# Counts, normalising steps and probabilities moved to ScalarE, and select() interleaved two tiles at a time with pair 0

## The chip, the cores and the metric

The kernel runs on one core of a Trainium2 chip. The metric is the device time of one launch in microseconds. A core has five engines that run side by side, each with its own instruction queue, worked off in order: TensorE (PE; its weight loads are PEld), VectorE (DVE), ScalarE (ACT), GpSimd (POOL) and SyncE (SP), which issues the DMAs. An instruction that waits for a semaphore holds everything behind it in its own queue.

## The reference

The program is a decoder trunk of two layers over 1024 positions of 1024 channels, all in float32. In each layer one projection of the normalised, modulated input is split into a convolution branch and an attention branch:

```
p = h @ w_in[l]
u_val, u_gate, g_conv, c_q, c_kv, k_idx, w_idx, g_attn = split(p)
y_conv = conformer_conv(...) * silu(g_conv)     # gate, causal conv of width 31, layer norm, silu, @ w_pw2
y_attn = dsa_attention(...) * silu(g_attn)
x = x + gate * rmsnorm(concat(y_conv, y_attn) @ w_out[l])
```

In the attention, an indexer gives every query t a score for every key s ≤ t. The 256 keys of the highest score are kept (of equal ones those with the lower position), and 8 heads attend to these alone:

```
_, sel = lax.top_k(score, 256)
logits = q . kv[sel] / sqrt(128) + rel_bias[t5_bucket(t - sel)]
o = softmax(logits) @ kv[sel]
```

## The kernel before

**Top 256 by bisection.** The 1024 queries are 8 tiles of 128. The first two have at most 256 keys and keep them all. For the other six, called j = 0 to 5, with 384, 512, 640, 768, 896 and 1024 keys, `topk` finds the 256th highest score of each query bit by bit. The upper half of a score's bits lies as int16 in `pl`. `search` tries a candidate per bit and counts the keys on one side of it: the counts of j = 1, 3, 5 on DVE (L559: 512, 768 and 1024 keys), those of j = 0, 2, 4 on ACT (L554, a Sign whose sum is the count). POOL then takes the step to the next candidate (L549, L562, L564, L566). Search 1 has 15 bits, search 2 has 16. Between them is the mid-search: for each tile, DVE counts the keys above the found upper half (L586) and puts the lower half of those equal to it in `pl` (L588), and the counts are added to the threshold `thr` (L592). L602 on ACT puts the scores back in place.

**Flags.** `select(j)` makes of the found value `tf` the mask of the kept keys, in place of the scores: greater (L608) and equal (L612), a running count of the equal ones (L613), those within the number needed (L614), all on DVE; their sum on POOL (L615) and the final 0 or −BIG on ACT (L616).

**Beside search 2**, PE works through products in an order written by hand: gate projections `g`, the transposes `zt` of the normalised convolution output, the pointwise products `pw`, `v`, and the queries `uq`. The other engines serve it: DVE takes the statistics (L693) and normalises `An` (L720, 32 tiles of 128x128, after a power on POOL, L717, that comes eight times for four tiles each); ACT applies silu to `zt` (L764, `sl`) and to the gates (L742); `sl` is split into a rounded high part `silh` (L767, a cast on DVE) and the rest `sill` (L768, POOL); DVE multiplies the pointwise products by the gate, `yc` (L786). Weights are split into high and low parts by ACT (L132) and by POOL or DVE (L133).

**Attention.** `attention` goes through four pairs of heads. A pair has four blocks c of two query tiles i = 2c, 2c+1: for each head e of the pair, `probs` makes logits (PE `lg`), takes a maximum with bias and mask (DVE L843, L847), the exponential and its sum (ACT L850), the reciprocal (DVE L851), and the multiplication by it (POOL L852). PE transposes the result (L865), ACT and DVE empty PSUM (L870, L872), and PE multiplies with `v` (`av`, L893, its end taken over by DVE in L896). `select(0)` to `select(3)` stand ahead of the attention in program order, `select(4)` and `select(5)` behind blocks c = 0 and c = 1 of pair 0. Tiles i = 0 and 1 need no flags; tile i needs those of j = i − 2.

**What sets the order.** PE's order is written by hand. The queues of the other engines come from a scheduler that builds them ahead of the launch from the program order and its own clock. Within search 2 a small planner, `Pace`, keeps a clock of DVE (`pace[0].free`): each helper operation registers its duration and the earliest place (`pace[0].op(..., us, lag)`, `pace[0].pe(us)` for PE's progress), and each count of L559 asks `pace[0].count` behind which of them it must be issued. So a helper operation that no longer registers moves the counts' places too. The queues are fixed at launch.

## Time and profile before

| | |
|---|---|
| three runs, median (lowest to highest) | 1235.27 us (1234.69 to 1236.12) |
| the profiled execution | 1234.0 us, of which the span of the records is 1232.2 us |
| PE busy in the span | 1173.8 us (95%) |
| DVE, ACT, POOL busy | 897.0, 701.9, 606.5 us |
| search 2 | layer 0: 262 to 353 us; layer 1: 861 to 954 us |
| pair 0, from the first flag to its last `av` | layer 0: 353.4 to 423.4 us; layer 1: 954.6 to 1025.7 us |

The span runs from the first to the last record; 1.8 us of the execution lie around it. An engine counts as busy while one of its instructions runs, also where it is slowed by another engine. Line numbers are those of the kernel before.

### The profile page before, as it was taken

The page shows a single profiled execution, that of the slowest core. Times are in us where ns is not written, and L with a number is a line of the kernel's source. Part 1 is how long each engine was busy: PE and PEld are TensorE (multiplying, and loading weights), DVE is VectorE, ACT ScalarE, POOL GpSimd, SP SyncE. Part 2 cuts the span into 40 slices and gives each one's busy share as a digit, 9 for nine tenths or more (in the row PEclk, how much of TensorE's full clock was granted, in tenths as well). Part 3 has the DMA queues.
Part 4 walks back from the last instruction along what each step waited for, and adds up shares of the span by engine and source line. Part 5 has one row for each costly group of instructions (what it writes and reads, how often), then busy time and mean ns, then how long its engine had stood idle before and what let it go on. Part 6 is the DMA issues. An engine that isn't in the chain of part 4 may idle for free.

```text
span 1232.2 us, 23069 instructions
## 1 busy us (share of the span) xinstructions
PE 1173.8 (95%) x7832; PEld 975.8 (79%) x7832; DVE 897.0 (73%) x2182; ACT 701.9 (57%) x1616; POOL 606.5 (49%) x1218
## 2 busy tenths in 40 slices
PE   6999999999987999999999999999999599999998
PEld 3788888877875777789989888888798377777998
DVE  4657788898798656757686688898888876667214
ACT  4545767766864556643254376785687355566221
POOL 4431136547548548635483211553864665685222
PEclk9999999999998999999999999999999699999999
DMA  9520258852100001148651122894111000021205
GB/s 352 201 85 18 69 195 274 275 171 75 35 27 1 9 10 47 33 127 292 235 196 34 46 52 74 270 289 160 58 30 43 1 10 5 6 77 63 76 18 189
DMA packets 93158, 130.20 MB, mean 106 GB/s; under 512 B 41576, under 2 KB 70768, under 8 KB 93040
## 3 DMA queue, kind: packets, MB, share of 16 engines
q1 hardware_dynamic: 93040, 128.73, 32.5%
q8 instruction: 62, 1.02, 0.3%
q14 instruction: 56, 0.46, 0.1%
HBM read 115.06 MB, written 13.64 MB: 104 GB/s over the span
## 4 chain that ended last, share of the span: by engine, by line
PE 85%; DVE 5%; POOL 5%; issue 2%; ACT 1%; DMA 1%; SPq 0%; DVEq 0%; POOLq 0%; ACTq 0%
PE av L893 7%; PE pt L865 5%; PE ixs L476 5%; PE u L112 5%; PE u L113 5%; PE u L114 5%; PE g L112 5%; PE g L114 4%; PE g L113 4%; PE o L112 4%; PE o L113 4%; PE o L114 4%; PE lg L112 3%; PE cv L674 2%; PE lg L113 2%; PE lg L114 2%
## 5 line engine op out<-in xcount | busy, mean ns | idle before, releaser
L559 DVE TENSOR_SCALAR_CACHE_REDUCE jv<-pl,cand 128x768 int8<-128x768 uint16 (+1 forms) x186 | 187.9, 1010 | 30.8 <-POOL cand L566 20.0
L554 ACT ACTIVATE ja<-pl,cand 128x896 int8<-128x896 uint16 (+1 forms) x186 | 154.1, 829 | 60.6 <-POOL cand L566 45.7
L850 ACT ACTIVATE p<-p,mx 128x128 f32<-128x128 f32 (+7 forms) x128 | 98.7, 771 | 57.1 <-DVE mx L847 49.1
L852 POOL TENSOR_SCALAR p<-p,ri 128x128 f32<-128x128 f32 (+7 forms) x128 | 99.6, 784 | 39.6 <-DVE ri L851 39.2
L133 POOL TENSOR_TENSOR wul<-raw,wuh 128x342 fp32r<-128x342 f32 (+1 forms) x48 | 46.9, 1000 | 129.3 <-ACT wuh L132 123.3
L112 PE MATMUL o<-woh,yh 128*128 128x256 f32 x384 | 109.5, 286 | 0.0
L114 PE MATMUL o<-woh,yl 128*128 128x256 f32 x384 | 108.6, 283 | 0.0
L113 PE MATMUL o<-wol,yh 128*128 128x256 f32 x384 | 108.1, 282 | 0.0
L865 PE MATMUL pt<-ident,p 128*128 128x128 f32 x576 | 94.4, 282 | 10.2 <-POOL p L852 7.7
L112 PE MATMUL u<-hT,wuh 128*128 128x512 f32 x256 | 101.4, 396 | 0.0
L112 PE MATMUL g<-hT,wgh 128*128 128x512 f32 x256 | 101.2, 395 | 0.0
L114 PE MATMUL u<-hT,wul 128*128 128x512 f32 x256 | 100.0, 391 | 0.0
L113 PE MATMUL u<-hT,wuh 128*128 128x512 f32 x256 | 99.9, 390 | 0.0
L113 PE MATMUL g<-hT,wgh 128*128 128x512 f32 x256 | 99.8, 390 | 0.0
L114 PE MATMUL g<-hT,wgl 128*128 128x512 f32 x256 | 99.7, 389 | 0.0
L837 POOL TENSOR_TENSOR p<-tb,score 128x256 f32<-128x256 f32 x96 | 75.5, 793 | 47.4 <-PE pt L865 47.3
L893 PE MATMUL av<-pt,v 128*64 128x256 f32 (+1 forms) x640 | 94.9, 372 | 1.9 <-DVE pt L872 1.8
L112 PE MATMUL lg<-kvT,q 128*128 128x384 f32 (+2 forms) x192 | 78.5, 410 | 18.3 <-DVE mx L847 18.2
L865 PEld LDWEIGHTS pt<-ident,p 128*128 128x128 f32 x576 | 67.8, 142 | 33.6 <-issue 13.6
L490 DVE SCALAR_TENSOR_TENSOR score<-relu,widx,score 128x384 f32<-128x384 f32 (+2 forms) x84 | 78.8, 976 | 18.8 <-ACT relu L482 18.1
L482 ACT ACTIVATE relu<-ixs 128x512 f32<-128x512 f32 (+2 forms) x140 | 66.7, 523 | 35.8 <-PE ixs L476 35.4
L966 ACT ACTIVATE ja<-o 128x256 int8<-128x256 f32 x64 | 24.5, 383 | 107.2 <-PE o L114 107.0
(294 smaller groups left out, 3439.7 us busy)
## 6 DMA issues: line engine op xcount, KB each, us to landing
wt<-in_wl_dram SPq DMA_DIRECT2D x64, 512.0 KB, 5.7
wa<-in_w_mod_dram SPq DMA_DIRECT2D x32, 512.0 KB, 4.9
raw<-in_w_in_dram SPq DMA_DIRECT2D x64, 171.0 KB, 2.7
wa<-in_w_ada_dram SPq DMA_DIRECT2D x16, 512.0 KB, 10.1
raw<-in_w_out_dram SPq DMA_DIRECT2D x32, 171.0 KB, 2.7
raw<-in_w_in_dram SPq DMA_DIRECT2D x32, 170.0 KB, 2.7
ad<-A SPq DMA_DIRECT2D x8, 512.0 KB, 3.7
at<-ad SPq DMA_DIRECT2D x16, 256.0 KB, 5.1
```

Source lines behind the costliest of these rows:

```text
L112: T.matmul(o, ah, bh, start=first, stop=False)
L113: T.matmul(o, ah, bl, start=False, stop=False)
L114: return T.matmul(o, al, bh, start=False, stop=last)
L482: S.activation(r[:, c0:c1], o[:, :c1 - c0], AF.Relu)
L490: V.scalar_tensor_tensor(acc, r[:, :w], wc, acc, op0=OP.mult, op1=OP.add)
L554: S.activation(ja[:, :wid(j)], src, AF.Sign, scale=-1.0, bias=col(cand, c), accum_out=col(ct_, c))
L559: V.tensor_scalar(jv[:, :wid(j)], src, col(cand, c), None, op0=OP.is_lt, op1=OP.add, accum_out=col(ct_, c))
L837: G.tensor_tensor(nb, tb, sc[:, OFF[i] + n0:OFF[i] + w], op=OP.add)
L850: mark[0] = S.activation(p[:, :w], p[:, :w], AF.Exp, scale=-1.0, bias=m[:, 2:3], accum_out=ri[:, 0:1])
L852: mark[1] = G.tensor_scalar(p[:, :w], p[:, :w], ri[:, 1:2], 1.0, op0=OP.mult, op1=OP.mult)
L865: T.transpose(t[:, 128 * j:128 * j + 128], p[:, 128 * (j0 + j):128 * (j0 + j) + 128], ident)
L893: T.matmul(o[64 * e:64 * e + 64, t0:256], lh, pts[e][j // 4][:, j % 4, t0:256], start=j == 0, stop=j == 2 * c + 1)
```

## The change

Seven edits, in both layers:

1. In the mid-search the six counts go from DVE (L586) to ACT, as a Sign with a bias `nhi` that POOL makes of the found value; POOL turns the sums into counts (six small operations), and the planner's clock is set 8 instead of 13 us ahead.
2. Of the 32 normalising steps `An` every second one goes from DVE to ACT, without a registration with the planner.
3. The 8 casts `silh` go from DVE to ACT, without a registration.
4. In pair 0, the multiplication by the reciprocal goes from POOL to ACT (`early`); the other pairs keep POOL.
5. `select(2)` and `select(3)` are called behind block c = 0 of pair 0, `select(4)` and `select(5)` behind c = 1.
6. The first half of the split of `w_uq` (`wuql`, three operations) goes from DVE to POOL.
7. Ahead of the attention only `select(0)` and `select(1)` stand.

```diff
@@ -581,16 +581,18 @@
 
         pace[0].start(12.0)
         hi = search(pl, by_group(thr, "thg"), 15)
+        nhi = small(name="nhi")
+        G.tensor_scalar(nhi, hi, -1.0, -0.5, op0=OP.mult, op1=OP.add)
         for j in range(6):
             src = pl[:, OFF[j + 2]:OFF[j + 3]]
-            V.tensor_scalar(jv[:, :wid(j)], src, col(hi, j), None, op0=OP.is_gt, op1=OP.add,
-                            accum_out=col(cnt, j))
+            S.activation(ja[:, :wid(j)], src, AF.Sign, bias=col(nhi, j), accum_out=col(cnt, j))
             V.scalar_tensor_tensor(src.bitcast(U16), src, col(hi, j), word(seg(j), 0),
                                    op0=OP.is_equal, op1=OP.mult)
-        for j in ACT_TILES:
-            V.tensor_scalar(col(cnt, j), col(cnt, j), 2.0, None, op0=OP.mult)
+        for j in range(6):
+            f = 1.0 if j in ACT_TILES else 0.5
+            G.tensor_scalar(col(cnt, j), col(cnt, j), f, f * wid(j), op0=OP.mult, op1=OP.add)
         V.tensor_tensor(thr, thr, cnt, op=OP.add)
-        pace[0].free += 13.0
+        pace[0].free += 8.0
         lo = search(pl.bitcast(U16), by_group(thr, "thg"), 16)
         th = small(I32, "th")
         V.tensor_copy(word(th, 1), hi)
@@ -717,8 +719,11 @@
             G.tensor_tensor(rs[:, ts], va[:, ts], mhalf[:, 0:4], op=OP.pow)
             V.scalar_tensor_tensor(nm[:, ts], m[:, ts], -0.125, rs[:, ts], op0=OP.mult, op1=OP.mult)
             for t in range(t0, t0 + 4):
-                pace[0].op(V.tensor_scalar(An[:, t, :], An[:, t, :], rs[:, t:t + 1], nm[:, t:t + 1],
-                                           op0=OP.mult, op1=OP.add), 0.38, 2.5 + 0.3 * t0)
+                if t % 2:
+                    S.activation(An[:, t, :], An[:, t, :], AF.Identity, scale=rs[:, t:t + 1], bias=nm[:, t:t + 1])
+                else:
+                    pace[0].op(V.tensor_scalar(An[:, t, :], An[:, t, :], rs[:, t:t + 1], nm[:, t:t + 1],
+                                               op0=OP.mult, op1=OP.add), 0.38, 2.5 + 0.3 * t0)
         yield
 
     def gate_w(l, gi, cblk):
@@ -764,7 +769,7 @@
                     S.activation(f[:, e].rearrange("p (t b) -> p t b", t=4), te[:, e], AF.Silu,
                                  scale=lg[:, 0, e:e + 1], bias=lg[:, 1, e:e + 1])
                 bs = slice(128 * hb, 128 * hb + 128)
-                pace[0].op(V.tensor_copy(hi[:, :, bs], f), 0.45, 5.0)
+                S.activation(hi[:, :, bs], f, AF.Copy)
                 G.tensor_tensor(lo[:, :, bs], f, f32(hi[:, :, bs]), op=OP.subtract)
             pace[0].pe(0.8)
             return hi, lo
@@ -815,7 +820,7 @@
             nc.sync.dma_start(tb, td[h])
             return qt, tb
 
-        def probs(q, tb_, i):
+        def probs(q, tb_, i, early):
 
             w = P * (i + 1)
             o = []
@@ -849,7 +854,10 @@
             ri = st("ri", [P, 2], name="ri", bufs=8)
             mark[0] = S.activation(p[:, :w], p[:, :w], AF.Exp, scale=-1.0, bias=m[:, 2:3], accum_out=ri[:, 0:1])
             V.reciprocal(ri[:, 1:2], ri[:, 0:1])
-            mark[1] = G.tensor_scalar(p[:, :w], p[:, :w], ri[:, 1:2], 1.0, op0=OP.mult, op1=OP.mult)
+            if early:
+                S.activation(p[:, :w], p[:, :w], AF.Copy, scale=ri[:, 1:2])
+            else:
+                mark[1] = G.tensor_scalar(p[:, :w], p[:, :w], ri[:, 1:2], 1.0, op0=OP.mult, op1=OP.mult)
             return p
 
         turn = [0]
@@ -882,7 +890,7 @@
                 for e in range(2):
                     for ii in range(2):
                         i = 2 * c + ii
-                        p = probs(*cur[e], i)
+                        p = probs(*cur[e], i, pr == 0)
                         transposed(p, i, ii, pts[e])
                 o = mm_ps("av")
                 for j in range(2 * c + 2):
@@ -900,7 +908,8 @@
                 if at in (1, 2) and pr < 3:
                     nxt.append(queries(2 * pr + 2 + (at == 2)))
                 if pr == 0 and at < 2:
-                    select(4 + at)
+                    select(2 + 2 * at)
+                    select(3 + 2 * at)
                 elif pr == 3 and at < 3:
                     with tc.issue_after(late[0][-1]), tc.issue_after(late[1][-1]):
                         if at == 0:
@@ -1124,7 +1133,7 @@
             gate(6)
             sil.append(prepared(3))
             products(2, sil[2])
-            wq = [load_w(w_uq[l, :, 0:1024], 1024, "wuq", "w4", eng=V)]
+            wq = [load_w(w_uq[l, :, 0:1024], 1024, "wuq")]
             wv = load_w(w_uv[l], 512, "wv", "f")
             next(gw[7])
             products(3, sil[3])
@@ -1134,7 +1143,7 @@
             dump(f"yc{l}", yc)
             v = v_proj(l, kv, wv)
         select = topk(l, sc)
-        for j in range(4):
+        for j in range(2):
             select(j)
         w0, ys = attention(l, cq, kv, v, sc, ya, wq, select, yc)
         dump(f"ya{l}", ya)
```

Three places in the queues follow; names are those of the section on the kernel, "x4" is a row that comes four times.

**ACT in layer 0, from the first silu `sl` of the convolution on.** Before:

```order
L554 ACTIVATE ja,cg<-pl,cand 128x640
L554 ACTIVATE ja,cg<-pl,cand 128x384
L764 ACTIVATE sl<-zt,lg 128x128 x4
L742 ACTIVATE An<-g 128x512
L764 ACTIVATE sl<-zt,lg 128x128 x4
L554 ACTIVATE ja,cg<-pl,cand 128x896
L554 ACTIVATE ja,cg<-pl,cand 128x640
```

Now (L723 is the normalising step, L747 the gate's silu, L769 `sl`, L772 `silh`):

```order
L554 ACTIVATE ja,cg<-pl,cand 128x896
L723 ACTIVATE An<-An,lns 128x128 x8
L769 ACTIVATE sl<-zt,lg 128x128 x4
L747 ACTIVATE An<-g 128x512
L723 ACTIVATE An<-An,lns 128x128 x4
L772 ACTIVATE silh<-sl 128x4x128
L723 ACTIVATE An<-An,lns 128x128 x2
L769 ACTIVATE sl<-zt,lg 128x128 x4
L554 ACTIVATE ja,cg<-pl,cand 128x640
L723 ACTIVATE An<-An,lns 128x128 x2
```

Eight normalising steps stand ahead of the first four `sl`, six of the other eight ahead of the next four, and two `silh` between; the counts of 640 and 384 keys come behind the second four.

**DVE in layer 0, end of search 2**, from the last `yc` group of the convolution on. Before:

```order
L786 TENSOR_TENSOR yc<-pw,yc 128x8x32 x4
L559 TENSOR_SCALAR jv,cg<-pl,cand 128x768
L559 TENSOR_SCALAR jv,cg<-pl,cand 128x512
L559 TENSOR_SCALAR jv,cg<-pl,cand 128x1024
L596 CAST th<-res 128x6
L597 CAST th<-res 128x6
L599 TENSOR_TENSOR tf<-th,sg 128x6
L608 TENSOR_SCALAR gt,cnt<-score,tf 128x384
```

Now (L791 is `yc`, L598 and L599 the casts of the two halves of the found value, L601 `tf`, L817 the finishing of a query block `q`, L610 the first flag):

```order
L791 TENSOR_TENSOR yc<-pw,yc 128x8x32 x2
L559 TENSOR_SCALAR jv,cg<-pl,cand 128x768
L791 TENSOR_TENSOR yc<-pw,yc 128x8x32 x2
L559 TENSOR_SCALAR jv,cg<-pl,cand 128x512
L559 TENSOR_SCALAR jv,cg<-pl,cand 128x1024
L559 TENSOR_SCALAR jv,cg<-pl,cand 128x768
L559 TENSOR_SCALAR jv,cg<-pl,cand 128x512
L559 TENSOR_SCALAR jv,cg<-pl,cand 128x1024
L598 CAST th<-res 128x6
L817 SCALAR_TENSOR_TENSOR q_4394<-uq,q_4393 128x512 x2
L599 CAST th<-res 128x6
L601 TENSOR_TENSOR tf<-th,sg 128x6
L610 TENSOR_SCALAR gt,cnt<-score,tf 128x384
```

Behind the first half of the `yc` group six counts are left instead of three, five of them behind the whole group; two blocks of `q` stand between the casts, ahead of `tf` and of the first flag. Before, the first `q` stood behind three tiles' first flags.

**DVE in layer 1, end of search 2**, again from the last `yc` group on. Before:

```order
L786 TENSOR_TENSOR yc<-pw,yc 128x8x32 x4
L559 TENSOR_SCALAR jv,cg<-pl,cand 128x512
L559 TENSOR_SCALAR jv,cg<-pl,cand 128x1024
L559 TENSOR_SCALAR jv,cg<-pl,cand 128x768
L559 TENSOR_SCALAR jv,cg<-pl,cand 128x512
L559 TENSOR_SCALAR jv,cg<-pl,cand 128x1024
L559 TENSOR_SCALAR jv,cg<-pl,cand 128x768
L559 TENSOR_SCALAR jv,cg<-pl,cand 128x512
L559 TENSOR_SCALAR jv,cg<-pl,cand 128x1024
L812 SCALAR_TENSOR_TENSOR q_11549<-uq,q_11548 128x512
L596 CAST th<-res 128x6
L812 SCALAR_TENSOR_TENSOR q_11549<-uq,q_11548 128x512
L597 CAST th<-res 128x6
```

Now:

```order
L791 TENSOR_TENSOR yc<-pw,yc 128x8x32 x2
L559 TENSOR_SCALAR jv,cg<-pl,cand 128x768
L791 TENSOR_TENSOR yc<-pw,yc 128x8x32 x2
L559 TENSOR_SCALAR jv,cg<-pl,cand 128x512
L559 TENSOR_SCALAR jv,cg<-pl,cand 128x1024
L598 CAST th<-res 128x6
L599 CAST th<-res 128x6
L601 TENSOR_TENSOR tf<-th,sg 128x6
L610 TENSOR_SCALAR gt,cnt<-score,tf 128x384
```

Three counts are left where there were eight, and no block of `q` stands ahead of the first flag any more; before, two stood beside the casts and a third behind `tf`.

## Rows read from the trace of the kernel before

**Rows 1.** The page: span, busy time and the chain's engines.

```profile
span 1232.2 us, 23069 instructions
PE 1173.8 (95%) x7832; PEld 975.8 (79%) x7832; DVE 897.0 (73%) x2182; ACT 701.9 (57%) x1616; POOL 606.5 (49%) x1218
PE 85%; DVE 5%; POOL 5%; issue 2%; ACT 1%; DMA 1%; SPq 0%; DVEq 0%; POOLq 0%; ACTq 0%
```

**Rows 2.** Windows (start:end, length, busy time and instructions by engine, clock, DMA).

```profile
core 0: us, PE busy (x) PEld busy (x) DVE busy (x) ACT busy (x) POOL busy (x), PEclk, DMA share, GB/s
353.40:367.20 13.80, 9.52 (x48) 7.82 (x46) 13.45 (x27) 8.27 (x13) 3.86 (x4) 1.00 0.01 2
367.20:423.40 56.20, 47.77 (x262) 34.55 (x263) 42.86 (x138) 27.97 (x64) 38.78 (x46) 0.88 0.02 6
423.40:463.20 39.80, 39.57 (x250) 29.27 (x249) 25.91 (x102) 21.62 (x49) 21.55 (x32) 1.00 0.03 8
889.50:954.60 65.10, 64.12 (x389) 57.12 (x388) 55.41 (x113) 52.25 (x125) 35.37 (x125) 1.00 0.13 37
954.60:967.80 13.20, 3.82 (x20) 2.91 (x18) 12.28 (x27) 5.32 (x8) 3.82 (x4) 0.75 0.00 1
967.80:1025.70 57.90, 50.25 (x262) 35.71 (x263) 44.25 (x137) 28.21 (x64) 38.64 (x46) 0.82 0.02 5
```

**Rows 3.** Waits (total us, times, longest): PE in 945:1027, POOL in 353:425.

```profile
PE lg L112 <- DVE mx L847: 12.2, 4, 9.4
...
POOL p L852 <- DVE ri L851: 6.9, 8, 2.8
```

**Rows 4.** Timeline of DVE, mid-search of layer 0 (start, length, instruction).

```profile
255.27 0.15 DVE L592 TENSOR_TENSOR thr<-thr,cnt 128x6 f32<-128x6 f32 x1
...
261.57 0.07 DVE L543 MEMSET cand<- 128x3 f32 x2
```

**Rows 5.** Lines by form, ACT and POOL (count, busy us, mean ns, idle before).

```profile
L554 ACT ACTIVATE ja<-pl,cand 128x640 int8<-128x640 int16 x30 | 24.8, 827 | 9.3 <-POOL cand L566 8.1
L554 ACT ACTIVATION_READ_ACCUMULATOR ja<-pl,cand 128x1 f32 x186 | 35.3, 190 | 0.0
L764 ACT ACTIVATE sl<-zt,lg 128x128 f32<-128x128 f32 x64 | 23.9, 462 | 7.2 <-PE zt L760 7.2
...
L717 POOL TENSOR_TENSOR lns<-lns,mhalf 128x4 f32<-128x4 f32 x16 | 15.9, 1034 | 0.1
```

**Rows 6.** Lines by form, DVE.

```profile
L720 DVE TENSOR_SCALAR An<-An,lns 128x128 f32<-128x128 f32 x64 | 24.2, 444 | 0.2
L767 DVE CAST silh<-sl 128x512 fp32r<-128x512 f32 x16 | 7.1, 446 | 0.8 <-ACT sl L764 0.8
L612 DVE TENSOR_SCALAR eq<-score,tf 128x640 f32<-128x640 f32 x2 | 3.1, 1554 | 1.2 <-POOL gt L615 1.2
...
L613 DVE TENSOR_TENSOR_SCAN score<-eq 128x768 f32<-128x768 f32 x2 | 5.6, 2816 | 0.0
L613 DVE TENSOR_TENSOR_SCAN score<-eq 128x896 f32<-128x896 f32 x2 | 4.0, 2010 | 0.0
```

**Rows 7.** Waits of PE in 262:300.

```profile
PE zt L760 <- ACT sl L764: 1.6, 1, 1.6
```

**Rows 8.** Timeline of DVE, end of search 2 in layer 0.

```profile
345.98 2.39 DVE L786 TENSOR_TENSOR yc<-pw,yc 128x256 f32<-128x256 f32 x4
350.20 1.28 DVE L559 TENSOR_SCALAR_CACHE_REDUCE jv<-pl,cand 128x1024 int8<-128x1024 uint16 x1
352.97 0.18 DVE L597 CAST th<-res 128x6 uint16<-128x6 f32 x1 [1.37 <-POOL res L570]
```

**Rows 9.** Timeline of DVE, end of search 2 in layer 1.

```profile
939.87 2.39 DVE L786 TENSOR_TENSOR yc<-pw,yc 128x256 f32<-128x256 f32 x4
949.76 1.28 DVE L559 TENSOR_SCALAR_CACHE_REDUCE jv<-pl,cand 128x1024 int8<-128x1024 uint16 x1 [0.15 <-DVE jv L559]
954.02 0.69 DVE L812 SCALAR_TENSOR_TENSOR q<-uq,q 128x512 fp32r<-128x512 f32 x1
```

## The prediction

> **What bounds the kernel now.** I read the page first: PE is busy 1173.8 of 1232.2 us and the chain of waits lies on PE for 85%, on DVE and POOL for 5% each [rows 1]. So the change, which touches no work of PE, can gain at most the 58 us in which PE has nothing to do, and I looked for where these lie. The table by stage answers that [rows 2]: in layer 0, between the first flag at 353.4 and the last `av` of pair 0 at 423.4, PE is busy 9.52 of 13.8 us and then 47.77 of 56.2 us, part of it at a lower granted clock (0.88 on the mean), so it lies idle 12.7 us there. In layer 1 it is busy 3.82 of 13.2 and 50.25 of 57.9 us, idle 17.0 us. Pair 1 is PE's own again: 39.57 of 39.8 us.
>
> What is late there is DVE. Pair 0 with the flags takes 70.0 us against 39.8 of pair 1, that is 30.2 more; DVE's busy time in the same stretches is 13.45 + 42.86 = 56.3 against 25.9 us, 30.4 more [rows 2]. The two differences agree: the stretch is as long as pair 1 plus DVE's work on the flags. The waits say the same: PE's largest, 12.2 us in four pieces (9.4 the longest), is for the maximum that DVE delivers [rows 3]. So two things count: when search 2 ends, for the flags start there, and how long DVE takes from the first flag to pair 0's later blocks. Beside search 2 PE is full (64.12 of 65.1 us in layer 1, [rows 2]), so time gained in the search is worth something only at its end, where PE runs out of products.
>
> **The change part by part**, against the profiled execution of 1234.0 us (span and 1.8 us around it), which is 1.3 us under the median of 1235.27.
>
> *Mid-search counts.* DVE loses six counts, but the threshold now waits for ACT's: six at about 0.83 + 0.19 us [rows 5] are 6.1 us, with the `score` passes and a gate's silu among them in the queue. I take the threshold as ready when it is now, at 255.27 [rows 4]. What changes is that the candidates' reset stands ahead of the statistics instead of behind them: it ran at 261.57, 6.3 us after the threshold, and ACT and POOL wait for it. They may start that much sooner, yet a round of the search closes only with DVE's three counts, which stay behind the statistics. Bounds: −6.3 us (the whole head start) and +2 (ACT's chain of counts two counts late); I take −0.5 per layer, next to the row that DVE sets.
>
> *Normalising steps and high parts.* 16 steps at 24.2 / 64 = 0.38 us are 6.0 us per layer off DVE, 8 casts at 0.44 us another 3.5 [rows 6]. ACT gets them: 16 passes at 23.9 / 64 = 0.37 us, by the silu of the same tile [rows 5], are 6.0 us, the casts about 4. The eight powers of POOL, 1.0 us each [rows 5], still set the pace of the normalising. New is where ACT does it: eight steps, 3.0 us, stand in its queue ahead of the first four `sl`, and six more ahead of the next four. PE's second four `zt` wait for the first `sl`, now 1.6 us [rows 7]. Half of the eight lie in the time in which ACT waits for POOL's powers anyway, so I take PE as 1.4 us later per layer; bounds 0 (all hidden) and +4 (all eight and part of the six on the path).
>
> *Where the counts stand*, layer 0. The last `yc` group starts at 345.98, when PE's product is there, not when DVE is free. Behind it three counts took 351.48 − 348.37 = 3.1 us, 1.04 each [rows 8]. The planner no longer sees the moved steps and puts fewer counts ahead: six stand behind the first half of the group, five behind the whole. That is 2.5 more, +2.6 us, and DVE's released 9.5 us are spent waiting for PE. With PE's 1.4 us the search ends 4.0 later. The two `q` blocks that now stand between the casts take 1.4 us, which the second cast waits for POOL anyway (1.37 us, [rows 8]); cost 0 there (up to +3 if PE's `uq` or ACT's part is late), and they no longer stand among the flags: −1.4.
>
> Layer 1: eight counts behind the last `yc` took 951.04 − 942.26 = 8.8 us, 1.10 each [rows 9]. Three and two are left: 5.5 fewer, −6.0 us. DVE must have done these before, 6.0 us in the 9.5 that it is released of. PE's 1.4 us go against it, and a `q` block of 0.69 us ahead of the first flag [rows 9] is gone: −0.7. ACT is the doubt: 52.25 of 65.1 us busy [rows 2], and with about 4 us of high parts in some 60 us it is 94% full; each round needs its counts too. I add +1.5.
>
> *Flags and pair 0.* The sum of DVE's flags until the fifth and sixth tile is the same; only their order changes, so the first maximum comes sooner by about 5 us of flags but the later ones meet the rest. What can go is time that DVE loses beside POOL: the 640-wide `eq` took 1.55 us where a 512-wide pass takes 0.45, so by size 0.56; the 768-wide scan took 2.82 where the 896-wide took 2.01, by size 1.72 [rows 6]. That is 2.1 us in two instructions. POOL is busy 38.78 of 56.2 us in this stretch [rows 2] and is rid of 16 of its operations. I take −3 per layer; bounds 0 and −6.
>
> By the Trainium skill ("SBUF — State Buffer", section "SBUF: two separate sides") VectorE and GpSimd share one pair of ports, which whoever starts first keeps for its whole instruction while the other stands still. The 1.55 and 2.82 us agree with that. But by this rule the sums `gt` that POOL keeps would hold up DVE as before, and more often where two tiles' flags stand next to each other; that is the fourth case below.
>
> *Normalising on ACT.* POOL waited 6.9 us, eight times, for the reciprocal [rows 3], and nobody behind it minded. ACT now waits in its place, with the next exponential and PE's evictions behind it, and the reciprocal stands in DVE's queue behind a scan. ACT itself has room: 8.27 + 27.97 of 70.0 us busy [rows 2], and 16 passes at 0.83 at most add 13. I take +1.2 per layer; bounds 0 and +6.9.
>
> Sum: mid-search −1.0; layer 0: +2.6 + 1.4 − 1.4 − 3.0 + 1.2 = +0.8; layer 1: −6.0 + 1.4 − 0.7 + 1.5 − 3.0 + 1.2 = −5.6. Together −5.8 us: 1228.2 us in the profiled execution's terms, and with its distance to the median 1229.5 us.
>
> **The rivals.**
>
> *First, all of it shows.* `zt` isn't late, ACT's reciprocal waits are hidden, and the flags give 5 us a layer: −1.0; layer 0 +2.6 − 1.4 − 5 = −3.8; layer 1 −6.0 − 0.7 − 5 = −11.7. Together −16.5, 1218.8 us. For it: PE's 17.0 idle us in layer 1 have room. Against: the flags' sum on DVE stays.
>
> *Second, no change.* ACT is the bound of search 2 in layer 1: the five and a half counts move ahead in the queue, but each round waits for ACT, so that the 4.6 us (6.0 − 1.4) don't come. 5.8 − 4.6 leaves −1.2, 1234.1 us. For it: 94%. Against: ACT now waits 9.3 us for POOL's candidates in 30 counts of one tile [rows 5].
>
> *Third, slower.* ACT's wait for the reciprocal in pair 0. If all 6.9 us lie on the path in both layers, the term is +6.9 instead of +1.2 twice, +11.4: +5.6, 1240.9 us. It decides from 4.1 us per layer, where it eats the gain. For it: ACT's queue is in order and feeds PE by the next exponential. Against: the first reciprocals are the ones behind scans, later ones follow at once.
>
> *Fourth, the ports.* If each of the six sums on POOL costs DVE 1.0 us, as the one behind the 640-wide `eq` did, the term is 6.0 − 2.1 = +3.9 instead of −3.0 per layer: +13.8 − 5.8 = +8.0, 1243.3 us. For it: that row [rows 6]. The Trainium skill's page named above gives the rule that speaks for it. Against: POOL's sums are as many as before, and the 896-wide scan shows no such loss beside the 768-wide one [rows 6].
>
> **How the numbers follow.** A change of less than 0.2%, 2.5 us, can't be told from none: faster is below 1232.8, slower above 1237.7 us. The forecast has 0.42 (own range 1226 to 1233), the first rival 0.15, the second 0.20, the third 0.17, the fourth 0.06. Faster: 0.42 + 0.15 and a little of the second, 0.60; slower: 0.17 + 0.06, less what of it ends within the bound, 0.22; the same 0.18. The range that holds 8 in 10 goes from the first rival's to the third's time, 1219 to 1241; the unknown ends (mid-search −6.3, ports) lie at its edges.
>
> **What the profile after would show.** Right: the first flag of layer 1 some 4 to 5 us sooner against the layer's start, that of layer 0 about 4 us later against its own; PE's `zt` waits near 3 us; PE's waits for maxima in layer 1 well under 12 us; pair 0 with the flags 2 or 3 us shorter than 70 and 71. Wrong: DVE idle between counts for POOL's candidate while ACT is at its own count (second case); waits of ACT for the reciprocal above 4 us per layer (third); `eq` and scans longer than before by their size (fourth). What would make the prediction wrong outright is a wait that the order doesn't show, above all at the head of pair 0.

## The result, and the profile after

The changed kernel takes 1242.45 us in the median of 4 runs (1241.75 to 1243.56), beside 1235.69 us of the kernel before: 1.0056 of it, with a 95% interval of 1.0039 to 1.0074. It is slower by 6.8 us, 0.56%, and 13 us over the forecast of 1229.5. The profiled execution took 1242.35 us with a span of 1240.6 us, 8.4 us over that of before.

The page of the changed kernel, span and busy times:

```profile
span 1240.6 us, 23039 instructions
PE 1181.3 (95%) x7832; PEld 978.9 (79%) x7832; DVE 870.9 (70%) x2098; ACT 751.1 (61%) x1720; POOL 587.1 (47%) x1206
```

To [rows 1]: DVE has 26 us less to do, ACT 49 us more, and PE, whose work is the same, is busy 7.5 us longer. The rows below show stretches of that work at a lower granted clock.

PE of the changed kernel in layer 0, around the transposes `zt` (start, length, instruction, in brackets the idle time before it and what ended it):

```profile
283.44 0.77 PE L765 MATMUL zt<-ident,An 128*128 128x128 f32 x4
288.20 1.12 PE L765 MATMUL zt<-ident,An 128*128 128x128 f32 x4 [3.99 <-ACT sl L769]
...
289.54 0.63 PE L113 MATMUL g<-hT,wgh 128*128 128x512 f32 x1
...
302.71 1.03 PE L765 MATMUL zt<-ident,An 128*128 128x128 f32 x8
```

The second and the third group of `zt` in the kernel before:

```profile
285.14 0.66 PE L760 MATMUL zt<-ident,An 128*128 128x128 f32 x4 [1.60 <-ACT sl L764]
...
297.33 1.03 PE L760 MATMUL zt<-ident,An 128*128 128x128 f32 x8
```

ACT of the changed kernel there:

```profile
282.95 3.81 ACT L723 ACTIVATE An<-An,lns 128x128 f32<-128x128 f32 x8 [2.21 <-DVE lns L720]
286.67 1.48 ACT L769 ACTIVATE sl<-zt,lg 128x128 f32<-128x128 f32 x4
```

POOL's eight powers, and ACT's first eight steps in layer 1:

```profile
281.67 7.88 POOL L719 TENSOR_TENSOR lns<-lns,mhalf 128x4 f32<-128x4 f32 x8
...
885.89 3.18 ACT L723 ACTIVATE An<-An,lns 128x128 f32<-128x128 f32 x8
```

The eight normalising steps (L723) stand ahead of the first four `sl` and last 3.81 us, so `sl` starts at 286.67 instead of 283.58, and PE waits 3.99 us where it waited 1.6 [rows 7]. In layer 0 ACT's own speed doesn't set these 3.81 us. Each of POOL's powers, 0.98 us apart, releases two of ACT's steps, and such a pair takes ACT 0.88 us: the first pair starts at 282.95, the fourth at 285.88. The first four `sl` need the tiles of the first power only, but in ACT's queue they stand behind steps that wait for the second, third and fourth. In layer 1 ACT came late to the same eight steps and did them without a gap in 3.18 us. What comes behind the wait is the second half of the price. The table by stage of the changed kernel (columns as in rows 2):

```profile
core 0: us, PE busy (x) PEld busy (x) DVE busy (x) ACT busy (x) POOL busy (x), PEclk, DMA share, GB/s
283.00:288.00 5.00, 1.10 (x12) 0.47 (x4) 3.94 (x16) 4.70 (x12) 5.00 (x6) 0.83 0.33 110
288.00:293.00 5.00, 4.80 (x14) 3.94 (x15) 4.62 (x11) 5.00 (x14) 4.04 (x9) 0.50 0.00 0
293.00:298.00 5.00, 5.00 (x28) 3.56 (x27) 2.00 (x6) 4.08 (x11) 2.43 (x4) 0.99 0.01 3
886.00:891.20 5.20, 1.06 (x6) 0.34 (x3) 4.15 (x17) 5.20 (x15) 5.20 (x6) 0.93 0.00 0
891.20:897.00 5.80, 5.73 (x16) 4.67 (x17) 3.17 (x8) 5.80 (x16) 5.30 (x11) 0.50 0.32 93
```

From 288 to 293 us the granted clock is 0.50, that is 1.2 of 2.4 GHz, and 14 of PE's instructions take the time in which 28 run right behind; the product at 289.54 takes 0.63 us where the same one takes 0.40 at the full clock (shown below for the third experiment). From the second to the third group of `zt` 14.5 us pass instead of 12.2. Layer 1 has the same picture: a wait of 4.1 us, then 0.50. Together PE reaches the third `zt` group 5.4 us late in layer 0 (302.71 for 297.33) and another 5.8 late in layer 1 (905.50 for 891.66, of which 8.0 came from layer 0). The kernel before stayed at 1.00 behind its wait of 1.6 us.

DVE of the changed kernel at the end of search 2, layer 0:

```profile
352.46 1.27 DVE L791 TENSOR_TENSOR yc<-pw,yc 128x256 f32<-128x256 f32 x2
...
358.24 1.28 DVE L559 TENSOR_SCALAR_CACHE_REDUCE jv<-pl,cand 128x1024 int8<-128x1024 uint16 x1
...
360.37 1.29 DVE L817 SCALAR_TENSOR_TENSOR q<-uq,q 128x512 fp32r<-128x512 f32 x2 [0.75 <-ACT q L816]
...
362.00 0.61 DVE L610 TENSOR_SCALAR_CACHE_REDUCE gt<-score,tf 128x384 f32<-128x384 f32 x1
```

and layer 1:

```profile
955.26 1.25 DVE L791 TENSOR_TENSOR yc<-pw,yc 128x256 f32<-128x256 f32 x2
...
957.30 1.28 DVE L559 TENSOR_SCALAR_CACHE_REDUCE jv<-pl,cand 128x1024 int8<-128x1024 uint16 x1
...
960.55 0.61 DVE L610 TENSOR_SCALAR_CACHE_REDUCE gt<-score,tf 128x384 f32<-128x384 f32 x1
```

To [rows 8, 9]: the first flag of layer 0 comes at 362.00 instead of 353.38, that of layer 1 at 960.55 instead of 954.63.

Pair 0 by its four blocks, from the first flag on (layer 0), and block c = 2 of layer 1, in the changed kernel:

```profile
362.00:380.50 18.50, 11.88 (x58) 8.51 (x56) 18.32 (x46) 10.57 (x25) 8.12 (x8) 0.94 0.00 0
380.50:400.00 19.50, 14.54 (x62) 10.24 (x63) 18.81 (x42) 9.42 (x19) 10.74 (x9) 0.79 0.00 0
400.00:420.80 20.80, 18.58 (x108) 13.58 (x107) 12.12 (x53) 19.40 (x34) 6.42 (x8) 1.00 0.05 14
420.80:431.40 10.60, 9.88 (x69) 6.68 (x70) 6.78 (x26) 4.52 (x13) 4.21 (x9) 1.00 0.01 2
1004.50:1024.10 19.60, 17.78 (x106) 13.83 (x107) 12.07 (x52) 18.91 (x32) 5.80 (x8) 1.00 0.05 15
```

Block c = 2 of the kernel before, layer 0:

```profile
397.05:412.60 15.55, 15.55 (x96) 12.09 (x97) 9.46 (x42) 10.58 (x20) 10.25 (x14) 1.00 0.06 17
```

To [rows 2]: the first `av` comes 18.5 us behind the first flag instead of 30.3, the second 38.0 instead of 43.7, as the order promised. But c = 2 takes 20.8 us instead of 15.5, with ACT (the fourth busy time of a row) at work in 19.40 of them, where it had 10.58 of 15.55 us and PE was full. At the end of pair 0, 69.4 us have passed for 70.1; in layer 1 it is 73.7 for 71.1. In layer 1 PE's waits for the maxima have gone down as forecast, from 12.2 to 5.1 us [rows 3], and the time came back in c = 2. The waits of PE there (total, times, longest):

```profile
PE lg L112 <- DVE mx L852: 5.1, 4, 1.6
PE av L901 <- DVE pt L880: 3.0, 2, 2.6
```

### The profile page after: what moved, and what is told of

The parts are those of the page before. It is cut to its first block, busy times and chain, and to the rows that moved or that the text cites. A ratio compares the mean times of both kernels' runs of the same rounds, so it can differ in the third digit from the quotient of the medians.

```text
span 1240.6 us, 23039 instructions
## 1 busy us (share of the span) xinstructions
PE 1181.3 (95%) x7832; PEld 978.9 (79%) x7832; DVE 870.9 (70%) x2098; ACT 751.1 (61%) x1720; POOL 587.1 (47%) x1206
## 5 line engine op out<-in xcount | busy, mean ns | idle before, releaser
L554 ACT ACTIVATE ja<-pl,cand 128x896 int8<-128x896 uint16 (+1 forms) x186 | 154.3, 830 | 43.7 <-POOL cand L566 38.4
L842 POOL TENSOR_TENSOR p<-tb,score 128x256 f32<-128x256 f32 x96 | 75.9, 797 | 70.1 <-PE pt L873 69.0
L112 PE MATMUL g<-hT,wgh 128*128 128x512 f32 x256 | 103.1, 403 | 0.0
L113 PE MATMUL g<-hT,wgh 128*128 128x512 f32 x256 | 101.5, 396 | 0.0
L490 DVE SCALAR_TENSOR_TENSOR score<-relu,widx,score 128x384 f32<-128x384 f32 (+2 forms) x84 | 79.0, 977 | 18.8 <-ACT relu L482 18.1
L860 POOL TENSOR_SCALAR p<-p,ri 128x128 f32<-128x128 f32 (+3 forms) x96 | 71.7, 750 | 35.5 <-DVE ri L856 35.2
```

Source lines behind the costliest of these rows:

```text
L112: T.matmul(o, ah, bh, start=first, stop=False)
L113: T.matmul(o, ah, bl, start=False, stop=False)
L490: V.scalar_tensor_tensor(acc, r[:, :w], wc, acc, op0=OP.mult, op1=OP.add)
L554: S.activation(ja[:, :wid(j)], src, AF.Sign, scale=-1.0, bias=col(cand, c), accum_out=col(ct_, c))
L842: G.tensor_tensor(nb, tb, sc[:, OFF[i] + n0:OFF[i] + w], op=OP.add)
L860: mark[1] = G.tensor_scalar(p[:, :w], p[:, :w], ri[:, 1:2], 1.0, op0=OP.mult, op1=OP.mult)
```

## The experiments

The theories named in the expectations: A, the steps on ACT hold back `sl`, PE waits and its clock falls; B, ACT's load alone; C, ACT full in c = 2 and 3; F, the flags cost DVE the same wherever they stand. Times are medians; a ratio is to the kernel before, run on the same chip, with its 95% interval, and versions are compared by their ratios. What is said of single stretches comes from one profiled execution of each version.

**Steps back on DVE** (`e1_norm_dve`).

```diff
-                if t % 2:
-                    S.activation(An[:, t, :], ..., AF.Identity, ...)
-                else:
-                    pace[0].op(V.tensor_scalar(An[:, t, :], ...), 0.38, 2.5 + 0.3 * t0)
+                pace[0].op(V.tensor_scalar(An[:, t, :], ...), 0.38, 2.5 + 0.3 * t0)
```

> The changed kernel, but all 32 normalising steps on DVE again and registered with the planner. Theory A (the steps on ACT hold back sl; PE waits 4.0 us for it and its clock falls to 0.50 for some 5 us): PE's zt wait is 1.6 us again, the granted clock stays 1.00 there, PE's third zt group comes about 5 us sooner in each layer; the counts go back ahead of the last yc group too. About 1230 us, 1227 to 1234. Rival B (ACT's load in search 2 and pair 0 sets the time, the wait is covered by slack before the search ends): the zt wait is gone but the first flags stay where they are; 1239 to 1243 us.

1234.21 us, 0.9996 (0.9982 to 1.0010): 0.6% under the changed kernel, 0.2 us above A's range. Third `zt` at 298.10, first flag of layer 0 at 349.71, 12.3 us sooner, so B falls. But the edit also puts the counts back ahead of the last `yc`, and pair 0 of layer 0 then takes 75.4 us; so it doesn't price the wait alone. The third experiment comes closer to that.

**Reciprocal's multiplication back on POOL** (`e2_pool_probs`).

```diff
-                        p = probs(*cur[e], i, pr == 0)
+                        p = probs(*cur[e], i, False)
```

> The changed kernel, but the multiplication by the reciprocal stays on POOL in pair 0. Theory C (in blocks c = 2 and 3 of pair 0 ACT is busy without a gap and sets the pace): ACT no longer full there, block c = 2 takes about 15 to 16 us instead of 20.8, some 4 to 5 us less per layer; 1232 to 1235 us. Rival D (the flags on DVE set pair 0's length whoever normalises; POOL's work slows them): c = 2 shorter but c = 0 and 1 longer by as much, 1240 to 1245 us.

1239.52 us, 1.0032 (1.0020 to 1.0044). Faster than the changed kernel by 0.24%, less than C said, and the two intervals still touch. Block c = 2 took 18.7 us in layer 0, and 20.3 in layer 1, where it had taken 19.6: C's picture fits layer 0 alone. About half of the block's growth in layer 0 comes with the flags' order, not with ACT: with the flags two by two and the multiplication on POOL (the sixth experiment) PE is full there for 18.4 us, with 107 of its instructions in the block where the kernel before had 96:

```profile
394.38:412.79 18.41, 18.41 (x107) 14.37 (x106) 12.27 (x53) 13.20 (x25) 14.08 (x16) 0.94 0.06 15
```

**PE covered** (`e3_cover`).

```diff
             for hb in range(2):
+                if hb and between is not None:
+                    between()
                 t = tp_ps("zt")
...
-            sil = [prepared(0)]
+            sil = [prepared(0, cover)]    # cover: next(gw[4]) twice, taken from behind prepared(0)
```

> The changed kernel, but PE gets a quarter of a gate projection (2.8 us of products) between its first and second four zt; nothing else is moved by hand. Theory A: PE's wait falls from 4.0 to about 1.2 us, the clock does not fall, PE is 4 to 5 us sooner behind it in each layer, and the first flags with it; about 1233 us, 1230 to 1236. Rival B (ACT's load and the place of the counts make the search late): the wait goes, the first flags move by less than 2 us per layer; 1239 to 1243 us.

1236.30 us, 1.0004 (0.9994 to 1.0015), 0.52% or 6.4 us under the changed kernel and 0.3 us above A's range. PE there:

```profile
288.16 0.66 PE L767 MATMUL zt<-ident,An 128*128 128x128 f32 x4 [1.24 <-ACT sl L771]
...
288.89 0.40 PE L113 MATMUL g<-hT,wgh 128*128 128x512 f32 x1
```

and the table of its stretches, to be held against that of the changed kernel:

```profile
283.00:288.00 5.00, 3.71 (x20) 2.57 (x16) 3.93 (x16) 4.70 (x13) 5.00 (x6) 1.00 0.36 117
288.00:293.00 5.00, 4.84 (x28) 3.51 (x29) 4.62 (x11) 5.00 (x14) 4.01 (x9) 1.00 0.01 3
```

The second `zt` comes at the same 288.16; ACT is as busy as before the edit. Only PE had something to do meanwhile: the wait is 1.24 us, the clock 1.00, and the third group comes 5.0 us sooner, at 297.66. The first flag of layer 0 follows, 4.8 us sooner at 357.25. Up to there this shows A: it is PE's idleness and the clock behind it, not ACT's load.

Behind it the path is another than A said. In layer 0 pair 0 now takes 74.0 us and ends at 431.25, where it ended at 431.42: the gain is gone again. In layer 1 the scheduler puts five counts behind the last `yc` instead of two, so the first flag, counted from the end of pair 0 of layer 0, is only 0.9 us sooner; there the gain appears in pair 0, which is 4.6 us shorter, with PE some 4 us further in its own products when the flags start. The last experiment shows what takes the gain in layer 0.

**Both back** (`e4_both`): the diffs of the first two.

> The changed kernel without the normalising steps on ACT and without the multiplication by the reciprocal on ACT. If A and C hold and add, the gains of the two single ones add: about 1221 to 1226 us. If one of them only uncovers the other (rival): as the better of the two, 1230 us or above.

1231.58 us, 0.9971 (0.9960 to 0.9982). Faster than before, but not the 1221 to 1226 of the sum: the time lies in the rival's range, 2.6 us under the better of the two single ones. Layer 0's flags start at 351.66, sooner than in the kernel before, yet pair 0 takes 76.4 us there.

**Flags as before as well** (`e6_flags_back`).

```diff
-                    select(2 + 2 * at)
-                    select(3 + 2 * at)
+                    select(4 + at)
...
-        for j in range(2):
+        for j in range(4):
```

> The changed kernel without the normalising steps and the multiplication by the reciprocal on ACT, and with the flags called as before (four tiles ahead of the attention, one behind c = 0, one behind c = 1). Only the mid-search counts, the high parts and the first wuql split are left of the change. Theory F (the six tiles' flags are the same DVE work wherever they stand; called late, DVE has nothing to do in the time in which PE makes the first queries): layer 0, where the search ends early, keeps its start, about 350 us, and c = 2 ends some 59 us behind it instead of 65; 1226 to 1229 us. Rival G (the interleaving is worth what brings the first maximum sooner): slower than the kernel without the two ACT moves, 1233 us or above.

1228.36 us, 0.9941 (0.9928 to 0.9954): F as expected. DVE of the version without ACT moves, flags two by two, 361 to 371 us:

```profile
361.00:366.00 5.00, 5.00 (x27) 4.26 (x26) 2.44 (x10) 4.53 (x10) 0.85 (x2) 1.00 0.00 0
366.00:371.00 5.00, 4.45 (x23) 3.36 (x22) 2.91 (x10) 2.59 (x9) 0.89 (x3) 1.00 0.00 0
```

and with the flags as before:

```profile
361.00:366.00 5.00, 4.73 (x24) 3.67 (x23) 5.00 (x8) 3.08 (x4) 1.48 (x1) 1.00 0.00 0
366.00:371.00 5.00, 3.73 (x17) 2.45 (x16) 4.43 (x15) 3.94 (x11) 4.93 (x6) 1.00 0.01 2
```

In the first, DVE (third pair) is busy 5.35 of these 10 us, since `select(2)` and `select(3)` stand in its queue behind c = 0 and PE, busy 9.45 of the 10 us, still has products for the queries and `v` to make; in the second 9.43. The first has pair 0 in 76.4 us, the second in 69.6.

**Flags two by two alone** (`e7_flags_only`): the reverse of that diff, in the kernel before.

> The kernel before with the flags alone called two by two behind c = 0 and c = 1. Theory F: the first av of pair 0 comes some 10 us sooner, the third at the same time; within 2 us of the kernel before, 1234 to 1237. Rival G: pair 0 is 3 to 6 us shorter in each layer, 1224 to 1230 us.

1232.47 us, 0.9970 (0.9959 to 0.9980). Between F and G: layer 0 gains 0.7 us in pair 0, layer 1 3.1 (68.0 for 71.1), where the first flag comes 2.2 us later against the end of pair 0 of layer 0. F in its plain form falls. That it matters whether the flags start ahead of the queries is theory K, put to the test below.

**Steps on ACT alone** (`e8_norm_only`): edit 2 in the kernel before, with the counts where they were ahead of the later `yc` groups.

> The kernel before with every second normalising step on ACT alone; the counts stand where they stood ahead of the later yc groups. Theory A: PE waits about 4 us for sl in both layers, its clock falls to 0.50, PE's third zt group is 5 us late; the search's end follows in both layers; 1240 to 1246 us. Rival B (there is slack until the search ends): 1234 to 1238 us.

1239.29 us, 1.0024 (1.0013 to 1.0035). PE waited 2.9 and 2.5 us, less than the 4 expected: in layer 0 POOL's first power starts at 280.14, 1.5 us sooner than in the changed kernel, and `sl` with it. The clock fell all the same:

```profile
286.60:292.00 5.40, 5.33 (x15) 4.36 (x16) 5.09 (x14) 5.40 (x15) 4.11 (x10) 0.50 0.00 0
```

Third `zt` at 301.73, first flag of layer 0 at 357.77, both 4.4 us late; the end of pair 0 there is 4.1 us late. So A's way is there with edit 2 alone, though the time lies just under A's range.

**Multiplication on ACT alone** (`e9_early_only`): edit 4 in the kernel before.

> The kernel before with pair 0's multiplication by the reciprocal on ACT alone. Theory C (ACT full in blocks c = 2 and 3 of pair 0): c = 2 longer than 15.5 us by 2 to 4, 1237 to 1243 us. Rival H (the wait was POOL's contention with DVE's flags, and this frees it): pair 0 shorter, 1229 to 1234 us.

1235.85 us, 1.0003 (0.9993 to 1.0013): nothing, so neither C's range nor H's. With flags one by one c = 2 took 16.0 us in both layers, ACT busy in 15.3 and 15.7 of them. With the flags two by two ACT has nine exponentials and eight multiplications in c = 2 of layer 0; with the flags one by one it has seven and six, the others having been done ahead of the block. The flags' last step on ACT (L618 there) comes once in c = 2, 1.1 us, in both. So ACT's multiplication costs where the order of the flags packs more of the large tiles into one block.

**Mid-search counts alone** (`e10_mid_only`, edit 1) and **high parts alone** (`e11_silh_only`, edit 3), each in the kernel before.

> The kernel before with the mid-search counts alone on ACT. The version with only mid-search, high parts and first wuql split measured 7.6 us less than before. Theory I (the mid-search gives little, as forecast, 0.5 us per layer; the high parts off DVE give the rest): 1234 to 1236 us. Rival J (the candidates' reset ahead of the statistics and three more counts ahead of the last yc group give most of it): 1228 to 1232 us.

> The kernel before with the high parts silh alone on ACT. Theory I: most of the 7.6 us, 1229 to 1232 us. Rival J: 1234 to 1237 us, since DVE's released 3.5 us per layer end in waits for POOL's candidates.

1234.56 us, 0.9996 (0.9987 to 1.0004), and 1234.32 us, 0.9992 (0.9983 to 1.0000). As far as these go, I holds for the counts and J for the high parts. Neither gives the 7.6 us that both give with the `wuql` split moved; that split was not moved alone, nor the other two together. What the queues show of it: behind the last `yc` group of layer 0 both have two counts left, of layer 1 five and nine; the combined version has none and five, the kernel before three and eight. How the parts divide the rest isn't settled.

**The cover on the faster version** (`e12_back_cover`).

> The version with the flags called as before and without the two ACT moves (1228.4 us), with a quarter of a gate projection between PE's first and second four zt. If PE's wait there and the lower clock behind it (zt group two to three took 13.8 us in layer 0 there, 11.4 in layer 1) lie on the path: 2 to 4 us less, 1224 to 1227. If the search's end hides them: 1228 to 1230.

1233.53 us, 0.9987 (0.9979 to 0.9996), 0.46% or 5.7 us slower than without the cover. A miss, and a telling one: PE's third `zt` came 3.7 us sooner (296.65), but in the queues built for this version the last `yc` group stands ahead of more counts: two instead of none in layer 0, eight instead of five in layer 1. That the scheduler did so because it sees the product earlier is likely and not shown. DVE in layer 1 of the version without the cover:

```profile
938.33 1.24 DVE L788 TENSOR_TENSOR yc<-pw,yc 128x256 f32<-128x256 f32 x2
...
943.70 1.28 DVE L559 TENSOR_SCALAR_CACHE_REDUCE jv<-pl,cand 128x1024 int8<-128x1024 uint16 x1
```

and with it:

```profile
940.14 1.23 DVE L790 TENSOR_TENSOR yc<-pw,yc 128x256 f32<-128x256 f32 x2
...
949.25 1.27 DVE L559 TENSOR_SCALAR_CACHE_REDUCE jv<-pl,cand 128x1024 int8<-128x1024 uint16 x1
```

Five counts behind the group take 5.4 us, eight 9.2. Of this 2.4 us are left at the first flag of layer 1, counted from the end of pair 0 of layer 0, and pair 0 there takes 0.7 longer. In layer 0 the first flag came 1.2 us later and pair 0 took 2.3 longer.

**Two by two in layer 1 alone**, with the cover (`e13_cover_flags1`) and without (`e15_flags1`).

```diff
-                    select(4 + at)
+                    for j in ((2 + 2 * at, 3 + 2 * at) if l else (4 + at,)):
+                        select(j)
...
-        for j in range(4):
+        for j in range(2 if l else 4):
```

> As the one with the quarter projection, and in layer 1 alone the flags called two by two behind c = 0 and c = 1. Theory K (two by two costs where the flags start before PE's queries are there, layer 0, and gains where the queries wait for the flags, layer 1: -1.9 and -3.1 us there in the two pairs of runs): 2 to 3 us below its neighbour. Rival: the same or slower.

> The version with mid-search counts, high parts and first wuql split alone (1228.4 us), and in layer 1 alone the flags two by two behind c = 0 and c = 1. Theory K (two by two gains where the queries wait for the flags and costs where the flags start before the queries are there): 2 to 3 us less, 1225 to 1227 us. Rival: 1228 us or above.

1230.59 us, 0.9961 (0.9949 to 0.9973), 2.9 under its neighbour; and 1225.73 us, 0.9917 (0.9904 to 0.9931), the fastest version found, 9.5 us under the kernel before. K holds in both times, though in the second the intervals of the two neighbours just touch. The profiles are less clear: pair 0 of layer 1 is 3.0 and 1.6 us shorter than in the neighbour, but in the second its first flag comes 1.4 us later. And layer 0, called the same way in the first and its neighbour, ends 1.9 us apart in these two profiles, so differences of 2 us between two profiles say little by themselves.

**Cover and POOL together, on the changed kernel** (`e14_cover_pool`): the diffs of the second and third.

> The changed kernel with both: the quarter of a gate projection between PE's first and second four zt, and pair 0's multiplication by the reciprocal on POOL. If the wait for zt with its clock and ACT's load in pair 0 are the two causes and separate: 6.1 and 2.9 us less add up, 1233 to 1234 us. If ACT's load in pair 0 weighs more once the wait is gone (the third av of layer 0 came 23.0 us behind the second there): 1229 to 1232. If both gave the same time twice: 1236 us.

1230.69 us, 0.9959 (0.9946 to 0.9971). With the cover in place ACT's multiplication costs 0.45%, 5.6 us, twice what it cost without, as the second reading had it: c = 2 of layer 0 went from 23.0 to 18.1 us. The two causes make 12 us together, and without them the change is faster than the kernel before by 0.41%. By layers, with layer 1 counted from the end of pair 0 of layer 0:

| profiled, us | layer 0: first flag | end of pair 0 | layer 1: first flag | end of pair 0 |
|---|---|---|---|---|
| before | 353.4 | 423.4 | 531.2 | 602.3 |
| changed | 362.0 | 431.4 | 529.1 | 602.8 |
| multiplication on POOL | 362.9 | 431.5 | 527.2 | 599.3 |
| PE covered | 357.3 | 431.3 | 528.2 | 597.3 |
| both | 358.2 | 426.0 | 528.5 | 596.1 |

Of the 8.4 us that the change lost, 8.0 were lost in layer 0. There either remedy alone gains nothing by the end of pair 0, and both gain 5.4 us, so each cause by itself seems enough to hold that stage. Layer 1 came out even (602.8 for 602.3), and each remedy gains there by itself.

## Why the prediction was wrong

| step, us | forecast | profiled |
|---|---|---|
| layer 0: PE late behind `zt` | +1.4 | +5.4 |
| counts behind the last `yc` | +2.6 | +2.7 (5.8 for 3.1) |
| last count to first flag | 0 | +0.6 |
| first flag | +4.0 | +8.6 |
| pair 0 with the flags | −3.2 | −0.6 |
| layer 1: PE late behind `zt` | +1.4 | +5.8 |
| counts behind the last `yc` | −6.0 | −6.7 (2.1 for 8.8) |
| last count to first flag | −0.7 | −1.6 |
| ACT's load in search 2 | +1.5 | not seen apart |
| first flag, from its layer's start | −3.8 | −2.1 |
| pair 0 with the flags | −1.8 | +2.5 |
| both layers, and mid-search −1.0 | −5.8 | +8.4 |

**The step that failed first** is "I take PE as 1.4 us later per layer". Its size was wrong twice. The wait grew by 2.4 us in layer 0: the prediction counted ACT's time for the eight steps and took half of it as hidden, but it is POOL's second to fourth powers that `sl` waits for in its queue, 3.81 us for all eight steps. The price of a step itself was near: 0.42 us on the mean (32 in 13.5 us) for the 0.37 taken from `sl`. And the term had no clock in it: 2.3 us more came from products at 0.50, although the windows of before showed clocks of 0.88 to 0.75 where PE lay idle longer. Most of the remaining 0.7 us is a first `zt` group that starts later (283.44 for 282.89). The upper bound of 4 us lay under the 5.4 and 5.8 measured because the clock was left out. The Trainium skill ("TensorE: Matmul & The Clock Gate", section "HAM oscillation — how this bites in real kernels") says that a gap between bursts throws PE back to the lower clock, so that the next burst starts cold. The rows above agree, and the covered version shows both halves of the price go.

**The second** is the price of normalising on ACT in pair 0, "+1.2 per layer", and it has another mechanism than the one priced. ACT waited for the reciprocal only 3.5 us, four times, in both layers (the line of the multiplication, L858, in the changed kernel):

```profile
its engine sat idle before it (us, times) until:
  DVE ri L856: 3.5, 4
```

The third rival named the right side and nearly the time (1240.9), but by that wait; that it came close is luck. What cost was ACT's own work in one block: c = 2, where exponentials and multiplications of the large tiles fill 19.40 of 20.8 us. Part of that block's growth, 2.9 of 5.3 us, came with the flags' order alone. "ACT itself has room", from 36 us in 70, was an average over blocks with different limits. Taken back in the changed kernel the multiplication gave 0.24%, and with PE covered 0.45%, 5.6 us for both layers.

**The third** is the flags' −3 per layer, for time that DVE loses beside POOL. That time didn't go. DVE's busy time in the flags' four kinds of passes is 54.6 us before and 54.0 after, both layers together, summed over their rows by form: the 640-wide `eq` fell from 1.55 to 0.55 us and the 768-wide scan from 2.82 to 2.11 [rows 6], but the 1024-wide pass behind the scan rose from 1.33 to 1.63, and others with it. (The 512-wide pass that the prediction scaled by takes 0.48 us, not 0.45.) DVE's lines by form in the changed kernel (count, busy us, mean ns, idle before):

```profile
L614 DVE TENSOR_SCALAR eq<-score,tf 128x640 f32<-128x640 f32 x2 | 1.1, 548 | 0.7 <-PE pt L873 0.7
...
L615 DVE TENSOR_TENSOR_SCAN score<-eq 128x768 f32<-128x768 f32 x2 | 4.2, 2114 | 0.0
...
L616 DVE SCALAR_TENSOR_TENSOR eq<-score,need,eq 128x1024 f32<-128x1024 f32 x2 | 3.3, 1634 | 0.0
```

The amount came all the same where the two causes above were taken away: pair 0 with the flags is 2.3 and 3.5 us shorter than before in the version with both remedies, with 54.8 us in these passes. So there the forecast's size was about right and its reason wrong. That the sooner first maximum gives it, which the prediction put at nothing, is likely, since PE's waits for the maxima in layer 1 fell; it isn't shown apart. The ports' rival did not come either: it asked for 3.9 us more than before in each layer, and the passes took no longer. No run took the sums off POOL, so what they hold up on DVE is not shown.

What was right: the counts' places behind the last `yc` (+2.7 and −6.7 for +2.6 and −6.0), read from the queues alone; the restart of the search behind the mid-search, at 261.71 for 262.04, a gain of 0.3 us (forecast 0.5); that this edit alone gives next to nothing (no difference clear of the noise); the sooner first maximum.

What stays open: without the terms for `zt` and for ACT's multiplication the forecast's sum is −11.0, and the version with both remedies gains only 4.5 us. Most of the difference lies ahead of the flags: its first flag comes 4.8 us later than before in layer 0 and 2.7 sooner in layer 1, where the forecast without `zt` has +2.6 and −5.2, and five counts stand behind the last `yc` of layer 1 there instead of the two that the forecast read. And why mid-search, high parts and `wuql` give 7.6 us together and 0.6 and 0.8 apart is shown only as far as the counts' places go.

## What to carry to other kernels

Before work is moved to an engine that "has room", look at what stands behind it in that engine's queue and feeds TensorE, and price a new idle time of TensorE together with the slow products behind it (1.6 to 2.9 us each time here). In an in-order queue ask also what the work put ahead is waiting for itself: here `sl` inherited the wait for three powers that it did not need. Cover such a wait with independent products rather than shorten it, and look again at the queues afterwards, since the scheduler may place other work differently: covered versions had up to three counts more behind the last `yc`. Two causes that hold the same stage hide each other; try the remedies together before calling one of them useless. Where a stage is set by one engine's fixed work, calling it later pays only if that engine isn't left idle in between: in the runs here it was in layer 0, and not in layer 1.

## What the runs showed of the hardware

TensorE's granted clock fell to 0.50 (1.2 of 2.4 GHz) behind waits of 2.9, 4.0 and 4.1 us, stayed at 1.00 behind 1.24 us in the covered kernel, and came back after some 5 us of products. From the second to the third `zt` group that cost 2.3 and 2.8 us behind the two waits of about 4 us, 2.9 and 1.6 behind those of 2.9 and 2.5. Behind a wait of 1.6 us it went either way. From 288 to 293 us of layer 0 the mean was 1.00 in the kernel before, with the steps back on DVE and with the high parts alone on ACT; it was 0.66 with both moves back, 0.74 with the flags as before as well, 0.80 with two by two in layer 1 alone on top of that, and 0.90 with the mid-search counts alone. So the length of the one wait doesn't tell the clock behind it.

A normalising step of 128x128 with a scale and a bias per partition, in place in SBUF, took ACT 0.49 us by itself and about 0.39 right behind another, 0.42 on the mean; DVE took 0.38 on the mean, and ACT 0.37 for the silu of the same size that reads PSUM.

DVE's flag passes took 54.0 to 55.2 us in five versions, whether POOL had pair 0's multiplications beside them or not.
